# Feed-forward weights kept in DRAM as split pairs: every second tile stored by the first token group, loaded by the second and third

## The chip, the cores and the metric

The kernel runs on one core of one Trainium2 chip. Its time is the device time of an execution in microseconds (us), given as the median of several runs. The core has five engines with a queue each: TensorE (PE, matmuls; the profile keeps its weight loads apart as PEld), VectorE (DVE), ScalarE (ACT), GpSimd (POOL) and SyncE (SP), which issues the transfers (DMAs) between DRAM and the on-chip memory. Each queue runs in order.

## The reference

One layer of a decoder trunk, in float32, over a prompt of 2048 tokens of width 1024 and 8 further samples of one token each. Cut to what matters:

```
h  = rmsnorm(x) * (1 + sc1) + sh1
qkv, z, ..., aq, ak, av, iq, ik, iw = split(h @ w_in)      # 3664 columns
o_gdn = gated delta rule over chunks (from qkv, z, ...)
o_att = attention over the 256 keys per query that an indexer (iq, ik, iw) picks
x  = x + ga1 * (concat(o_gdn, o_att) @ w_out)
h2 = rmsnorm(x) * (1 + sc2) + sh2
gate, up = split(h2 @ w_ffn_in)                            # 1024 x 5632
x  = x + ga2 * ((silu(gate) * up) @ w_ffn_out)             # 2816 x 1024
y  = rmsnorm(x)
```

## The kernel before, in words

**Split products.** The large products keep float32 accuracy by three passes in the faster format float32r: each operand is a pair, the rounded value (hi) and what the rounding lost (lo), and `mm3` (lines 178 to 182) adds hi·hi, hi·lo and lo·hi into one accumulator bank. A weight tile is 128 x 512. `weights` (lines 149 to 169) makes its pair: it loads the raw tile into a buffer `wr` (2 of them, 256 KB), ACT rounds it into the first half of a buffer `wi` (line 163, called the cast here), and DVE subtracts for the second half (line 164); the two together are called a conversion. `wi` has 3 buffers, so the pair for a tile can be made once PE has finished the tile three before it. Each tile gives PE 4 x 3 matmuls of 512 columns. Called with a key, `weights` also stores the finished pair in DRAM, 512 KB, under that key (lines 166 to 168), and on a later call with the same key loads the pair straight into `wi` (lines 153 to 155): no raw tile, no cast, no subtraction. Before the change only the input projection does so: 56 tiles, stored by the first group of tokens and loaded by the other three, 168 loads.

**Groups.** The prompt is cut into 4 groups of 512 tokens. `projects` runs the input projection of the four, with the delta rule beside it; then `ffn` runs once per group. It does the output projection (16 weight tiles, line 1858), the norm, and then for 11 blocks of 256 hidden columns the first feed-forward product (8 tiles each, line 1919, a tile from two raw loads of 128 KB) and, two blocks at a time, the second (44 tiles in all, line 1966): 148 tiles per group. After each run of tiles the four accumulator banks are drained: line 1769 and 1770 for the residual, lines 1934 to 1941 for the gated product. The names there: `d` is a bank, `tm` and `ca` scratch rows, `ah` and `al` the split product, `hh` and `hl` the split hidden rows. The fourth group carries the 8 samples as well (`samp`); its raw tiles are needed by a further matmul (line 1812), and they come from other buffers (`raw`, lines 1798 to 1802).

**What stands beside it.** While the feed-forward groups run, the rest of the attention runs on the same engines: the indexer's scores (line 1626 on PE, 1628 on ACT, 1635 on DVE), the selection (lines 1489 to 1521), softmax and values (lines 1671 to 1724), the loads of their K and V tiles (lines 1667 and 1696), and copies of the paged caches (line 622, on SP).

**What sets the order.** PE's order is written out by a small planner (`weave`, lines 491 to 514): it runs the streams (feed-forward, indexer, attention, samples) step by step, and chooses by an estimate of when DVE and ACT will be done, to which `weights` adds 0.76 and 0.62 for a conversion (line 165). The order of the other queues is made by the scheduler of the build from the resulting program; SP's order is among these.

Of the kernel before, what the change touches and what calls it, by code (L numbers as in the profile page):

```python
# [112 lines left out]
class K:  # L113
# [1637 lines left out]
    def ffn(self, g):  # L1751
# [44 lines left out]
        side, at, ring = deque(), [0, 0], [0]  # L1796
# [6 lines left out]

        def weights(src):
            if not samp:
                return (*self.weights(src), None)
            return self.weights(src, raw=raw)

        def beside(pq, x, wr, start, stop):
# [43 lines left out]
        for hf in range(2):  # L1853
            cs = slice(hf * 512, (hf + 1) * 512)
            pd = D4()
            pq = P("g") if samp else None
            for k in range(KB):
                wh, wl, wr = weights([A["w_out"][0, k * 128:(k + 1) * 128, cs]])
                if samp:
                    beside(pq, sx[:, k, :], wr, k == 0, k == KB - 1)  # L1860
                yield from three(pd, lambda t: oh[:, k, S(t)], lambda t: ol[:, k, S(t)], wh, wl, k, KB - 1)
            for t in range(4):
                gated_add(pd[t], row[:, cs], xt[:, t, cs], hf, t)
                self.squares(ms[:, t, hf:hf + 1], xt[:, t, cs])
            if samp:
                def out(pq=pq, hf=hf, ms=ms):
                    gated_add(pq[:, :128], rws[:, hf], xs[:, hf])
                    self.squares(ms[:, 4, hf:hf + 1], xs[:, hf])
                after(0, 0, out)
# [37 lines left out]
        for p0 in range(0, np_, per):  # L1907
# [5 lines left out]
            for pi, pr in enumerate(prs):  # L1913
# [3 lines left out]
                for k in range(KB):  # L1917
                    kr = slice(k * 128, (k + 1) * 128)
                    wh, wl, wr = weights([A["w_ffn_in"][0, kr, f0:f0 + 256], A["w_ffn_in"][0, kr, FF + f0:FF + f0 + 256]])
                    if samp:  # L1920
                        beside(pq, sx[:, k, :], wr, k == 0, k == KB - 1)
                    for j in range(4):
                        self.mm3(pd[j], wh[:, S(j)], wl[:, S(j)], hh[:, k, :], hl[:, k, :], k == 0, k == KB - 1)
                        yield 3 * MM, 0, bank(j, k, KB - 1, act=0.6)
                    yield from tick()
                    if not pr and k < KB - 2:
                        hidden(k + 2)
                        yield TP, 0, dict(dve=1.5, act=0.6, use="s", need="s" if k < KB - 3 else None)
# [31 lines left out]
            for hf in range(2):  # L1960
                cs = slice(hf * 512, (hf + 1) * 512)
                pd = D4()
                pq = P("g") if samp else None
                for b in range(nf):
                    fr = (p0 * 2 + b) * 128
                    wh, wl, wr = weights([A["w_ffn_out"][0, fr:fr + 128, cs]])
                    if samp:
                        beside(pq, ax[:, b, :], wr, b == 0, b == nf - 1)
                    yield from three(pd, lambda t: ah[b][:, S(t)], lambda t: al[b][:, S(t)], wh, wl, b, nf - 1)
                last = p0 + per >= np_  # L1970
                for t in range(4):
                    gated_add(pd[t], row[:, cs], xt[:, t, cs], last and hf, t)
                    if last:
                        self.squares(ms[:, t, hf:hf + 1], xt[:, t, cs])
                if samp:
                    def out(pq=pq, hf=hf, last=last, ms=ms):
                        gated_add(pq[:, :128], rws[:, hf], xs[:, hf])
                        if last:
                            self.squares(ms[:, 4, hf:hf + 1], xs[:, hf])
                    after(0, 0, out)  # L1980
# [37 lines left out]
```

## Time and profile before

| what | value |
| --- | --- |
| median of 3 runs | 3674.93 us (3673.78 to 3680.48) |
| the profiled execution, its own time | 3680.55 us |
| its span, first to last instruction | 3678.6 us |
| mean granted clock of TensorE | 0.965 |
| PE, DVE, ACT, POOL busy | 3429.4, 2090.6, 1475.8, 599.2 us |
| read from and written to DRAM | 435.49 MB and 124.75 MB |

The page gives busy time by engine and, for each group of like instructions (line, engine, operation, tiles written and read), their count, busy time, mean duration and the idle time of the engine just ahead of them, with what ended it. Further views of the trace list who waited for whom, busy time in chosen stretches of the span, and the instructions in order of time. Times in the timelines are microseconds from the start of the span. In a list of waits a row reads: the waiting engine, tile and line, what it waited for, us in total, times, longest. A rise of PE's busy time is not more work: matmuls overlap, and their durations are longer when the clock is granted at half.

### The profile page before, as it was taken

Reading aid. Unit: us, or ns where it says so; the run is one execution under the profiler, and the core shown is the slowest. Engines: PE = TensorE matmul, PEld = TensorE weight load, DVE = VectorE, ACT = ScalarE, POOL = GpSimd, SP = SyncE. Lnnn points to the kernel's source line nnn. Section 1 sums busy time; section 2 is a strip of 40 time slices with the busy share of each in tenths; the row PEclk is TensorE's granted clock in tenths of the full one; section 3 lists DMA queues with packets and bytes.
Section 4 is the critical chain, followed back from the end, with each engine's and each line's share of the span. In section 5 each row is a group of like instructions: output and inputs, shape, how many; then the busy total and the mean of one; then the engine's idle time right before and its main releaser. Section 6 shows DMA issues by size and latency. Waiting matters only on the chain.

```text
span 3678.6 us, 62998 instructions
## 1 busy us (share of the span) xinstructions
PE 3429.4 (93%) x23441; PEld 2649.0 (72%) x23441; DVE 2090.6 (57%) x4377; ACT 1475.8 (40%) x2868; POOL 599.2 (16%) x548
## 2 busy tenths in 40 slices
PE   7999999999998898999888999999899999899997
PEld 5867778777776776777665677787677777677775
DVE  3656646646644665666667555667666664443434
ACT  3333323323334333344456544564645543322222
POOL 0001000101001023212210122212022112221213
PEclk7999999999999898999998999999999999899998
DMA  6755575575676225455544453335433233432221
GB/s 246 244 204 164 180 243 175 184 241 167 193 262 205 70 94 157 124 167 161 158 153 130 127 174 113 114 98 177 138 91 99 90 103 107 169 107 80 78 82 64
DMA packets 412270, 545.52 MB, mean 148 GB/s; under 512 B 47364, under 2 KB 285225, under 8 KB 411946
## 3 DMA queue, kind: packets, MB, share of 16 engines
q1 hardware_dynamic: 411954, 541.41, 46.2%
q8 instruction: 186, 3.05, 0.3%
q14 instruction: 130, 1.06, 0.1%
HBM read 435.49 MB, written 124.75 MB: 152 GB/s over the span
## 4 chain that ended last, share of the span: by engine, by line
PE 74%; DVE 9%; DMA 7%; ACT 4%; issue 4%; SPq 1%; POOL 0%; DVEq 0%; ACTq 0%; POOLq 0%
PE d L180 18%; PE d L182 16%; PE d L181 16%; PE s L1626 3%; PE g L1688 3%; PE s L1671 2%; DVE wi L164 1%; PE g L1700 1%; DMA wi<-kept 1%; PE g L1812 1%; DMA wr<-in_w_ffn_out_dram 1%; DMA x_d<-xt 1%; PE g L1058 1%; ACT bias L1500 1%; ACT wi L163 1%
## 5 line engine op out<-in xcount | busy, mean ns | idle before, releaser
L180 PE MATMUL d<-hh,wi 128*128 128x512 f32 x1792 | 778.8, 435 | 24.0 <-DVE tm L1769 5.8
L181 PE MATMUL d<-hl,wi 128*128 128x512 f32 x1792 | 710.6, 397 | 7.0 <-DVE hl L415 5.8
L182 PE MATMUL d<-hh,wi 128*128 128x512 f32 x1792 | 710.6, 397 | 0.0
L164 DVE TENSOR_TENSOR wi<-wr,wi 128x512 fp32r<-128x512 f32 x537 | 402.7, 750 | 470.1 <-ACT wi L163 467.4
L163 ACT CAST wi<-wr 128x512 fp32r<-128x512 f32 x537 | 332.3, 619 | 784.5 <-PE d L182 499.2
L180 PEld LDWEIGHTS d<-hh,wi 128*128 128x128 f32 x1792 | 342.0, 191 | 120.9 <-issue 29.4
L182 PEld LDWEIGHTS d<-hh,wi 128*128 128x128 f32 x1792 | 341.6, 191 | 77.8 <-DVE wi L164 0.8
L181 PEld LDWEIGHTS d<-hl,wi 128*128 128x128 f32 x1792 | 343.1, 191 | 75.6 <-DVE hl L415 10.6
L180 PE MATMUL d<-wi,hh 128*128 128x512 f32 x768 | 324.7, 423 | 20.5 <-DMA wi<-kept 13.2
L180 PE MATMUL d<-wi,ah 128*128 128x512 f32 x704 | 301.2, 428 | 8.8 <-ACT ah L1940 5.6
L181 PE MATMUL d<-wi,hh 128*128 128x512 f32 x768 | 302.0, 393 | 1.0 <-DVE wi L164 1.0
L182 PE MATMUL d<-wi,hl 128*128 128x512 f32 x768 | 302.4, 394 | 0.0
L182 PE MATMUL d<-wi,al 128*128 128x512 f32 x704 | 282.2, 401 | 3.2 <-POOL al L1941 2.6
L181 PE MATMUL d<-wi,ah 128*128 128x512 f32 x704 | 282.2, 401 | 0.0
L1941 POOL TENSOR_TENSOR al<-ca,ah 128x512 fp32r<-128x512 f32 x88 | 119.1, 1365 | 844.9 <-ACT ah L1940 608.4
L1635 DVE SCALAR_TENSOR_TENSOR sc<-rl,iw,sc 128x512 f32<-128x512 f32 (+3 forms) x224 | 165.8, 740 | 81.5 <-ACT rl L1628 75.5
L1628 ACT ACTIVATE rl<-s 128x512 f32<-128x512 f32 (+3 forms) x288 | 150.3, 544 | 144.1 <-PE s L1626 136.6
L1770 POOL TENSOR_TENSOR xt<-xt,tm 128x512 f32<-128x512 f32 x96 | 136.5, 1436 | 411.5 <-DVE tm L1769 365.7
L180 PEld LDWEIGHTS d<-wi,hh 128*128 128x128 f32 x768 | 145.2, 189 | 68.7 <-DMA wi<-kept 17.0
L1626 PE MATMUL s<-ik,iqT 128*128 128x512 f32 (+3 forms) x576 | 170.8, 396 | 10.0 <-ACT rl L1628 9.7
L1500 ACT ACTIVATE bias<-sc,sv 128x640 bf16<-128x640 f32 (+11 forms) x120 | 169.7, 1414 | 22.8 <-DVE sv L1502 13.5
L180 PEld LDWEIGHTS d<-wi,ah 128*128 128x128 f32 x704 | 135.2, 192 | 52.6 <-issue 11.0
(532 smaller groups left out, 5587.5 us busy)
## 6 DMA issues: line engine op xcount, KB each, us to landing
wi<-kept SPq DMA_DIRECT2D x168, 512.0 KB, 3.4
wr<-in_w_ffn_in_dram SPq DMA_DIRECT2D x572, 128.0 KB, 2.3
wr<-in_w_ffn_out_dram SPq DMA_DIRECT2D x143, 256.0 KB, 2.6
kept<-wi SPq DMA_DIRECT2D x56, 512.0 KB, 3.4
xt<-in_x_prompt_dram SPq DMA_DIRECT2D x8, 2048.0 KB
row<-in_w_ada_dram SPq DMA_DIRECT2D x32, 512.0 KB, 4.3
wr<-in_w_in_dram SPq DMA_DIRECT2D x56, 256.0 KB, 3.6
kT<-kT_d SPq DMA_DIRECT2D x54, 256.0 KB, 3.0
```

What stands on the lines that cost most here:

```text
L163: nc.scalar.copy(w[:, 0], wr)
L164: nc.vector.tensor_tensor(w[:, 1], wr, w[:, 0].bitcast(F32), op=OP.subtract)
L180: self.o(nc.tensor.matmul(out, wh, xh, start=start, stop=False, **kw))
L181: self.o(nc.tensor.matmul(out, wh, xl, start=False, stop=False, **kw))
L182: self.o(nc.tensor.matmul(out, wl, xh, start=False, stop=stop, **kw))
L1500: nc.scalar.activation(c, s, AF.Sign, bias=t, accum_out=cnt)
L1626: self.o(nc.tensor.matmul(ps[:, :w], iq[:, h, :].bitcast(F32R), B["ikT"][c * 2 + a][:, :w].bitcast(F32R), start=a == 0, stop=a == 1))
L1628: nc.scalar.activation(r[:, :w], ps[:, :w], AF.Relu)
L1635: nc.vector.scalar_tensor_tensor(s, r[:, :w], iw, s, op0=OP.mult, op1=OP.add)
L1688: self.o(nc.tensor.matmul(po[:, :256], V[:, kb % 4, :], PT[:, b * 256:(b + 1) * 256], start=kb == 0, stop=kb == i))
L1770: (nc.vector if soon else nc.gpsimd).tensor_tensor(xt, xt, tm, op=OP.add)
L1941: nc.gpsimd.tensor_tensor(al[b], a, ah[b].bitcast(F32), op=OP.subtract)
```

## The change

The first, second and third feed-forward group count their weight tiles with `ring`. Tiles with an odd number, the first, third and so on, 74 of 148, now get a key that holds the number alone. The number runs anew in each group, and so the first group stores 74 pairs of 512 KB after their conversion, and the second and third load these 74 pairs each (148 loads in place of 148 raw tiles and their conversions). Tiles with an even number and the whole fourth group stay as they are. The loads and stores are issued on SP like the raw ones. Lines behind 1806 move by one.

```
         def weights(src):
             if not samp:
-                return (*self.weights(src), None)
+                ring[0] += 1
+                return (*self.weights(src, ("ffn", ring[0]) if ring[0] % 2 else None), None)
             return self.weights(src, raw=raw)
```

The change moves instructions on every engine, since a tile that is loaded as a pair adds nothing to the planner's estimate for DVE and ACT. On SP, in the third group, where the first feed-forward product has just begun: `wr` are raw tiles, `xt` the residual rows, `kept` a stored pair, the V and oT rows attention's. Before:

```order
L162 DMA wr<-in_w_ffn_in_dram 128x256 x6
L1930 DMA xt<-x_d 128x4x1024
L1696 DMA V<-V_d 128x4x128
L162 DMA wr<-in_w_ffn_in_dram 128x256 x4
L1696 DMA V<-V_d 128x4x128
L1724 DMA oTh_d<-PT 128x2x128
L162 DMA wr<-in_w_ffn_in_dram 128x256 x2
L1724 DMA oTl_d<-oT 128x2x128
L162 DMA wr<-in_w_ffn_in_dram 128x256 x6
L162 DMA wr<-in_w_ffn_out_dram 128x512 x7
```

and after:

```order
L162 DMA wr<-in_w_ffn_in_dram 128x256 x2
L154 DMA wi<-kept 128x1024
L1931 DMA xt<-x_d 128x4x1024
L1696 DMA V<-V_d 128x4x128
L162 DMA wr<-in_w_ffn_in_dram 128x256 x2
L1696 DMA V<-V_d 128x4x128
L154 DMA wi<-kept 128x1024
L1724 DMA oTh_d<-PT 128x2x128
L1724 DMA oTl_d<-oT 128x2x128
L162 DMA wr<-in_w_ffn_in_dram 128x256 x2
L154 DMA wi<-kept 128x1024
L162 DMA wr<-in_w_ffn_out_dram 128x512
```

Every second raw tile has given its place to the load of a pair, and attention's rows stand behind such loads as they stood behind raw ones. The second piece is DVE's queue in the third group, at the sixth of the eleven gated drains (`th` and `ca` two times each; `sc` are steps of the indexer). Before:

```order
L164 TENSOR_TENSOR wi<-wr,wi 128x512
L1935 SCALAR_TENSOR_TENSOR th<-th,d 128x512
L1635 SCALAR_TENSOR_TENSOR sc<-rl,iw,sc 128x512
L1937 SCALAR_TENSOR_TENSOR ca<-th,d 128x512
L1935 SCALAR_TENSOR_TENSOR th<-th,d 128x512
L1635 SCALAR_TENSOR_TENSOR sc<-rl,iw,sc 128x512
L164 TENSOR_TENSOR wi<-wr,wi 128x512
L1937 SCALAR_TENSOR_TENSOR ca<-th,d 128x512
```

and after:

```order
L164 TENSOR_TENSOR wi<-wr,wi 128x512
L1936 SCALAR_TENSOR_TENSOR th<-th,d 128x512
L1635 SCALAR_TENSOR_TENSOR sc<-rl,iw,sc 128x512 x2
L1938 SCALAR_TENSOR_TENSOR ca<-th,d 128x512
L1936 SCALAR_TENSOR_TENSOR th<-th,d 128x512
L1938 SCALAR_TENSOR_TENSOR ca<-th,d 128x512
```

The subtraction between the two products is gone, and both indexer steps stand ahead of the first. The third piece is DVE's queue in the second group, where the second half of the output projection is drained (`tm` and `ca`; `sv` and `sc` belong to a selection, `s` to the samples). Before:

```order
L1769 TENSOR_TENSOR tm<-d,row 128x512
L164 TENSOR_TENSOR wi<-wr,wi 128x512
L1769 TENSOR_TENSOR tm<-d,row 128x512
L1770 TENSOR_TENSOR xt<-xt,tm 128x512
L1769 TENSOR_TENSOR ca<-d,row 128x512 x2
```

and after:

```order
L1769 TENSOR_TENSOR tm<-d,row 128x512
L1633 SCALAR_TENSOR_TENSOR sc,sums<-rl,iw,sc 128x256
L1770 TENSOR_TENSOR xt<-xt,tm 128x512
L1489 TENSOR_REDUCE sv<-sums 128x1
L1492 TENSOR_TENSOR sc<-sc,cf 128x128
L1769 TENSOR_TENSOR tm<-d,row 128x512
L1490 TENSOR_SCALAR sv<-sv 128x1
L1493 MAX sv<-sc 128x8
L1769 TENSOR_TENSOR ca<-d,row 128x512
L1770 TENSOR_TENSOR xt<-xt,tm 128x512
```

The conversion has left this drain, and steps of the indexer and of a selection have come into it.

## Prediction

> **What bounds the kernel now.** First the top of the profile's page: which engine is full.
>
> ```profile
> span 3678.6 us, 62998 instructions
> PE 3429.4 (93%) x23441; PEld 2649.0 (72%) x23441; DVE 2090.6 (57%) x4377; ACT 1475.8 (40%) x2868; POOL 599.2 (16%) x548
> ```
>
> TensorE holds the span. It idles for 3678.6 - 3429.4 = 249 us, and only what shortens or adds such idling can move the end. So I cut the span at the feed-forward groups (the first matmul of each) and read busy time by stretch: the second to fourth projection, then the first, second and third feed-forward group.
>
> ```profile
> 318.00:1161.90 843.90, 787.11 (x8054) 623.39 (x8053) 464.55 (x1206) 284.60 (x695) 65.26 (x70) 0.98 0.62 202
> 1161.90:1873.70 711.80, 638.49 (x4567) 511.67 (x4565) 445.76 (x933) 285.30 (x552) 156.91 (x123) 0.93 0.46 138
> 1873.70:2520.50 646.80, 618.58 (x2889) 469.68 (x2887) 400.01 (x794) 336.57 (x583) 116.18 (x125) 0.98 0.42 129
> 2520.50:3142.90 622.40, 598.85 (x2627) 468.46 (x2625) 382.27 (x701) 307.88 (x504) 118.74 (x87) 0.98 0.37 115
> 1873.70:3142.90 1269.20, 1217.43 (x5513) 938.14 (x5511) 782.29 (x1494) 644.45 (x1087) 234.93 (x212) 0.98 0.39 122
> ```
>
> The columns are length, busy us of PE, PEld, DVE, ACT and POOL, granted clock, DMA share and GB/s. The conversions that the change takes away lie in groups two and three (last row), where PE idles for 1269.2 - 1217.4 = 51.8 us. That is all there is to win from waits. Next, what the conversions cost there, and who waits for them: the groups by line, and then the list of who waited for the subtraction's result.
>
> ```profile
> L164 DVE TENSOR_TENSOR wi<-wr,wi 128x512 fp32r<-128x512 f32 x293 | 226.5, 773 | 218.8 <-ACT wi L163 217.4
> L163 ACT CAST wi<-wr 128x512 fp32r<-128x512 f32 x294 | 181.8, 619 | 356.3 <-PE d L182 305.5 <-DMA wr<-in_w_ffn_in_dram 20.5 <-DMA wr<-in_w_out_dram 15.8
> ```
>
> ```profile
>   PEld d L180: 0.5, 2
>   PEld d L181: 0.5, 2
>   PEld d L182: 0.4, 1
> ```
>
> ACT itself idles 305.5 us ahead of the cast, for a tile that PE has not yet let go: the conversions run ahead of PE, and PE waits directly for them for next to nothing. They matter only as queue neighbours of other work. What PE does wait for in this stretch is the list of waits:
>
> ```profile
> PE g L1700 <- ACT big L1679: 11.1, 4, 5.3
> PE d L180 <- DVE ca L1937: 5.4, 5, 1.9
> PE d L181 <- DVE hl L415: 4.1, 3, 2.8
> PE d L180 <- DVE tm L1769: 4.0, 3, 2.8
> PE s L1671 <- DVE st L1672: 3.7, 4, 1.4
> PE d L182 <- POOL al L1941: 1.9, 2, 0.9
> ```
>
> These are the softmax (big) and, behind it, drains of the accumulator banks (ca, tm) and the hidden rows (hl), all short.
>
> **The change part by part.** *Removed:* 74 of 148 conversions in each of groups two and three, 148 in all: 148 x 0.619 = 92 us of ACT and 148 x 0.773 = 114 us of DVE. Both engines are under 63% busy there (782 and 644 of 1269 us), so of this only what stood ahead of something that PE waited for counts. One such place, from the timelines of POOL, DVE and PE:
>
> ```profile
> 2877.51 1.66 POOL L1941 TENSOR_TENSOR al<-ca,ah 128x512 fp32r<-128x512 f32 x1 [31.87 <-ACT ah L1940]
> 2877.96 1.76 DVE L164 TENSOR_TENSOR wi<-wr,wi 128x512 fp32r<-128x512 f32 x1
> 2879.64 0.67 DVE L1937 SCALAR_TENSOR_TENSOR ca<-th,d 128x512 f32<-128x512 f32 x1
> 2880.37 0.50 PE L180 MATMUL d<-wi,ah 128*128 128x512 f32 x1 [1.87 <-DVE ca L1937]
> ```
>
> A subtraction of 1.76 us stands ahead of the product ca, and PE waits 1.87 us for ca. The order of the changed kernel has no conversion there (the second piece in the section on the change). I went through all waits of PE over 0.3 us in the stretch in this way; there are 36, 48.6 us in all, the first and the last being
>
> ```profile
> 1897.28 0.50 PE L180 MATMUL d<-wi,hh 128*128 128x512 f32 x1 [0.90 <-DVE tm L1769]
> 3129.94 0.79 PE L182 MATMUL d<-wi,al 128*128 128x512 f32 x1 [0.93 <-POOL al L1941]
> ```
>
> and summed the part of each that the removed conversions fill on the engine waited for, during the wait or in the 3 us ahead of it, capped by the wait: 8.4 us. Counting the removed conversions on both engines gives 17.5 us. I take **-8.4**, since each wait names one engine; ends 0 and -17.5. The rest (softmax, selection) has no removed conversion near it.
>
> The subtraction above is over twice as long as its mean, 0.773 us, and overlaps POOL's own subtraction of 1.66 us. The Trainium skill, SBUF — State Buffer, "Who interferes with whom", says that a VectorE instruction with two SBUF inputs contends with a GpSimd instruction that reads SBUF; the row agrees. By that rule the removed subtractions would also free POOL, and PE's waits for al (1.9 us in the list of waits) could go: an estimate of -10.3 for this term in place of -8.4.
>
> *The clock.* A wait is followed by slow matmuls. Behind one of 2.77 us, with the stretch's granted clock below:
>
> ```profile
> 2004.35 0.80 PE L181 MATMUL d<-hl,wi 128*128 128x512 f32 x1 [2.77 <-DVE hl L415]
> 2004.95 0.63 PE L182 MATMUL d<-hh,wi 128*128 128x512 f32 x1
> 2004.00:2009.50 5.50, 5.15 (x12) 4.08 (x13) 5.50 (x16) 0.00 (x0) 0.00 (x0) 0.50 0.90 345
> ```
>
> The mean clock of 0.98 over 1269 us costs about 0.02 x 1269 = 25 us of work. In proportion to the waits (8.4 of 51.8), **-4**; ends 0 and -8.5 (17.5 of 51.8).
>
> *Added in groups two and three:* 148 loads of a 512 KB pair, each in place of a raw load of 256 KB. Issues and landings:
>
> ```profile
> wi<-kept SPq DMA_DIRECT2D x168, 512.0 KB, 3.4
> wr<-in_w_ffn_in_dram SPq DMA_DIRECT2D x572, 128.0 KB, 2.3
> kept<-wi SPq DMA_DIRECT2D x56, 512.0 KB, 3.4
> DMA to landing us min/median/max: 2.9/3.4/7.9
> ```
>
> A raw load waits only for the raw buffer, which the conversion frees early. A kept load goes straight into wi and waits on SP until PE has finished the tile three before. I followed the PE semaphore that each kept load and the rows ahead of it on SP wait for: apart from the very last load, none stands behind a row that waits for a later PE instruction than its own. Behind it on SP stand kT and V loads of attention; SP waits already, mostly for conversions that follow PE:
>
> ```profile
> SPq L162 <- DVE wi L164: 530.1, 220, 7.7
> SPq L1696 <- PE g L1688: 129.5, 36, 14.7
> ```
>
> So the head of the queue changes its reason to wait, not its pace. From the release to its use a kept tile has two tiles of matmuls. Where nothing lies between them, seven tiles take
>
> ```profile
> 3104.97:3124.03 19.06, 19.06 (x86) 15.76 (x84) 7.62 (x10) 4.36 (x7) 4.80 (x4) 1.00 0.34 99
> ```
>
> or 2.72 us each, so the window is at least 5.4 us against a landing of 3.4 us: 2.0 us spare, gone only when a landing is late. The projection is the nearest case: there all tiles of three groups are loaded so, at a DMA share of 0.62, and PE waited
>
> ```profile
> PE d L180 <- DMA wi<-kept: 14.6, 8, 4.0
> ```
>
> 14.6 us for 168 loads; at that rate 148 loads cost 12.9 us. The change adds 148 x 0.26 MB = 38.8 MB to 1269 us, 31 GB/s on 122, so the share stays near 0.5, and every second tile is still raw. I take a third, **+4**; ends 0 and +12.9.
>
> *Added in group one:* 74 stores of 512 KB; no conversion goes away. A store waits for its conversion on DVE, as the raw load two tiles on does already, and it holds the buffer wi until it has landed: 3.4 us against three tiles, 8.2 us. In the projection's first group 56 such stores stood one behind the other, and the tile kept<-wi is named in none of PE's waits. **+1**; ends 0 and +9.9, one more wait for SP's queue like group one's longest, which is
>
> ```profile
> PE g L1239 <- DMA qT<-qT_d: 9.9, 1, 9.9
> ```
>
> *Moved:* a loaded tile books no time on DVE and ACT with the planner (line 165 is not reached), so index and selection steps come somewhat earlier in groups two and three. In the third piece of the section on the change steps of the indexer and of a selection stand inside a drain where one conversion stood; its maximum takes 1.5 us, against 0.77 for a conversion:
>
> ```profile
> L1493 DVE MAX8 sv<-sc x12: 829/1546/2295, 1449.3 to 2915.9; 128x8 f32<-128x640 f32 x1, 128x8 f32<-128x768 f32 x1, 128x8 f32<-128x896 f32 x1, 128x8 f32<-128x1024 f32 x1
> ```
>
> Elsewhere it takes work out of drains. **+2**; ends -4 and +6, four such drains at 1.5 us, with the gain for the side on which steps leave a drain bounded by the 4.0 us of waits for tm.
>
> Sum: -8.4 - 4 + 4 + 1 + 2 = -5.4 us, so **-5**. The profiled execution took 3680.55 us (span 3678.6 and 1.95 around it), 5.6 above the median of the runs; the difference goes onto the median: 3674.93 - 5 = **3670**. About 0.2%, 7.3 us, is what a measurement of this kernel can tell from no change.
>
> **The rivals.** *The engines' queues count more than I allow (faster).* Half the conversions gone shorten each drain on both engines: -17.5, the clock's -8.5, then +4 and +1: -21, or **3654**. For it speaks that no conversion is left between the products of the second piece; against it, that most of the 48.6 us are softmax and selection with no conversion near. The Trainium skill, TensorE: Matmul & The Clock Gate, "Part 1: The HAM clock gate (the "warmup" mystery)", says the array's default is the half clock, and a busy window of about 3.4 us releases it; the slow rows behind the wait agree, and by it short waits that vanish would give back more than their own length. Chance 0.34.
>
> *Kept loads come late (slower).* Place: tiles loaded in groups two and three where matmuls run back to back. The price is the projection's rate, 12.9 us, in 8 x 148/168 = 7 waits; each puts PE at half clock for some 3.4 to 5.5 us (the row at 2004 shows 5.5), losing 1.7 us or more: 12 us. With the moved steps at +6, the stores at +1 and the gain of 8.4 without its clock: 12.9 + 12 + 6 + 1 - 8.4 = +23; with the moved steps at nothing +17, and I take that: **3692**. It decides once waits for wi<-kept, clock included, pass 8.4 + 4 + 7 = 19 us. For it speaks the maximum landing of 7.9 us against a window of 5.4; against it the lower DMA share. Chance 0.25.
>
> **How the numbers follow.** My forecast, within 7.3 us of no change, has 0.41, the faster rival 0.34, the slower one 0.25; so faster 0.34, same 0.41, slower 0.25. The likeliest case alone reaches from 3668 to 3682. The range goes on to both rivals, a little beyond the faster one and short of the slower one's full price: 3650 to 3690.
>
> **What would show it.** Right: waits for wi<-kept in groups two and three under 8 us; L164 down by 148 (537 to 389 on wr); PE's waits for ca, tm, hl and th lower by some 8 us; group one's length within 5 us of 711.8; the fourth group unchanged. Wrong: over 15 us of waits for wi<-kept, or PE waiting in group one for a conversion held up by a store; or, on the other side, idle time in groups two and three falling from 52 to under 30 us.

## The result, and the profile after

| | before | after |
| --- | --- | --- |
| median of 4 runs each | 3674.36 us (3669.31 to 3680.48) | 3703.93 us (3699.57 to 3706.17) |
| ratio after to before | | 1.0078, 95% interval 1.0062 to 1.0093 |
| span of the profiled execution | 3678.6 us | 3704.4 us |

The change makes the kernel slower by some 29 us, 0.8%. The forecast was -5, and the measured median lies above its range. The top of the page of after:

```profile
span 3704.4 us, 62595 instructions
PE 3427.9 (93%) x23441; PEld 2650.1 (72%) x23441; DVE 1980.8 (53%) x4229; ACT 1393.3 (38%) x2720; POOL 585.9 (16%) x548
```

DVE lost 110 us of work and ACT 82 (the prediction counted 114 and 92), and PE's busy time is the same within 2 us. So the 25.8 us between the two spans are idle time of PE. The same three feed-forward groups as in the prediction, by stretch (length, busy time of PE, PEld, DVE, ACT and POOL, granted clock, DMA share, GB/s):

```profile
1161.60:1894.69 733.09, 638.41 (x4566) 509.40 (x4565) 443.56 (x931) 283.90 (x550) 155.83 (x123) 0.93 0.58 186
1894.69:2548.40 653.71, 625.36 (x2933) 472.38 (x2932) 362.56 (x758) 306.72 (x532) 116.40 (x126) 0.99 0.50 160
2548.40:3168.63 620.23, 587.67 (x2584) 465.16 (x2582) 311.84 (x592) 256.50 (x412) 106.99 (x86) 0.97 0.44 143
```

Group one, which gained the stores and lost nothing, went from 711.8 to 733.1 us: +21.3, with PE busy for the same 638.4. Group two went from 646.8 to 653.7 and group three from 622.4 to 620.2, together +4.7. These two are best read together: some 44 matmuls have moved from group three into group two (2889 became 2933 there, and 2627 became 2584), and PE's busy time with them. Most of the loss is in group one. Its DMA share rose from 0.46 to 0.58. The groups of the conversion in the page of after:

```profile
L164 DVE TENSOR_TENSOR wi<-wr,wi 128x512 fp32r<-128x512 f32 x389 | 282.6, 727 | 505.2 <-ACT wi L163 479.4
L163 ACT CAST wi<-wr 128x512 fp32r<-128x512 f32 x389 | 240.9, 619 | 711.3 <-PE d L182 425.2
```

The count is the 389 that was foretold, and ACT still idles for PE (425.2 us): the conversions stayed ahead of it. What PE waited for in groups two and three of after (us in total, times, longest):

```profile
PE d L180 <- DMA wi<-kept: 9.8, 3, 7.3
...
PE d L181 <- DVE hl L415: 6.8, 4, 2.0
...
PE d L180 <- DVE ca L1938: 3.9, 3, 1.7
...
PE d L180 <- DVE th L1936: 2.8, 2, 1.5
...
PE d L180 <- DVE ca L1769: 1.9, 2, 1.4
...
PE d L180 <- DVE tm L1769: 1.0, 1, 1.0
```

The stored pairs came late 3 times. The wait for ca at the gated drains fell from 5.4 to 3.9 and that for tm from 4.0 to 1.0, but that for hl rose from 4.1 to 6.8. For group one, the longest entries of PE's waits in the second part of the group, 1395 to 1880, first in before:

```profile
PE g L1688 <- ACT PT L1703: 13.9, 4, 4.7
PE g L1239 <- DMA qT<-qT_d: 9.9, 1, 9.9
...
PE g L1294 <- DVE s L1289: 4.2, 2, 3.3
...
PE d L180 <- DVE tm L1769: 2.7, 4, 1.3
```

and in after:

```profile
PE g L1688 <- ACT PT L1703: 16.8, 3, 8.9
PE g L1239 <- DMA iqT<-iqT_d: 12.8, 1, 12.8
...
PE g L1294 <- DVE s L1289: 7.3, 4, 3.8
PE d L180 <- DVE tm L1769: 4.9, 5, 1.7
...
PE d L180 <- DVE st L1678: 3.7, 1, 3.7
```

One short wait is new, the last row (3.7 us, for a step of the softmax); the other rows are each some 2 to 3 us longer. No wait of PE in this window names a conversion or a stored pair. That picture fits many causes, so the runs below take them apart.

### The profile page after: what moved, and what is told of

It is laid out like the page before. It is cut to its first block, busy times and chain, and to the rows that moved or that the text cites. A ratio compares the mean times of both kernels' runs of the same rounds, so it can differ in the third digit from the quotient of the medians.

```text
span 3704.4 us, 62595 instructions
## 1 busy us (share of the span) xinstructions
PE 3427.9 (93%) x23441; PEld 2650.1 (72%) x23441; DVE 1980.8 (53%) x4229; ACT 1393.3 (38%) x2720; POOL 585.9 (16%) x548
## 3 DMA queue, kind: packets, MB, share of 16 engines
q1 hardware_dynamic: 409938, 619.00, 51.1%
## 4 chain that ended last, share of the span: by engine, by line
PE 74%; DMA 9%; DVE 8%; issue 3%; ACT 3%; SPq 2%; POOL 0%; DVEq 0%; ACTq 0%; POOLq 0%
PE d L180 18%; PE d L182 16%; PE d L181 16%; PE s L1626 3%; PE g L1688 3%; PE s L1671 3%; DMA wi<-kept 2%; DMA wr<-in_w_ffn_in_dram 2%; PE g L1700 1%; PE g L1813 1%; DVE wi L164 1%; PE g L1058 1%; DMA x_d<-xt 1%; ACT wi L163 1%; DMA wr<-in_w_ffn_out_dram 1%
## 5 line engine op out<-in xcount | busy, mean ns | idle before, releaser
L164 DVE TENSOR_TENSOR wi<-wr,wi 128x512 fp32r<-128x512 f32 x389 | 282.6, 727 | 505.2 <-ACT wi L163 479.4
L163 ACT CAST wi<-wr 128x512 fp32r<-128x512 f32 x389 | 240.9, 619 | 711.3 <-PE d L182 425.2
L1942 POOL TENSOR_TENSOR al<-ca,ah 128x512 fp32r<-128x512 f32 x88 | 118.4, 1356 | 912.4 <-ACT ah L1941 672.5
L1500 ACT ACTIVATE bias<-sc,sv 128x640 bf16<-128x640 f32 (+11 forms) x120 | 169.7, 1414 | 38.8 <-DVE sv L1502 19.0
```

Of the source, the lines that this page charges most:

```text
L163: nc.scalar.copy(w[:, 0], wr)
L164: nc.vector.tensor_tensor(w[:, 1], wr, w[:, 0].bitcast(F32), op=OP.subtract)
L1500: nc.scalar.activation(c, s, AF.Sign, bias=t, accum_out=cnt)
L1942: nc.gpsimd.tensor_tensor(al[b], a, ah[b].bitcast(F32), op=OP.subtract)
```

## The experiments

The theories, by the letters that the expectations use. **A**: the issues of the 74 stores crowd SP's queue. **B**: the bytes of the stores crowd the transfers. **C**: a store holds its buffer `wi` too long. **D**: the order of the instructions, which the change moved, is worse. All times are medians; "before" is run beside each kernel on the same chip. Group lengths are of the profiled executions.

**The stores alone, and the loads alone.** The stores of group one without any loads:

```
- ("ffn", ring[0]) if ring[0] % 2 else None
+ ("ffn", ring[0]) if ring[0] % 2 and not g else None
```

> The first group stores its 74 pairs, and nobody loads them: groups two and three convert all tiles as before. Theory A (SP's queue is full in the first feed-forward group, between about 1395 and 1840 us, because the page copies run there; each store issued on it puts back every load behind it): the first group is longer by some 20 us, as in the changed kernel, groups two and three are as before, total +18 to +25 us over before. Theory B (bytes: the stores' traffic makes the loads of the first group land later) and theory C (a store holds its buffer wi until it has landed, so the next conversions are late): the same +20. Theory D (the loss comes from the new order of index and selection steps that the planner makes once loaded tiles book no time): under +5 us, since here every tile books its time.

3699.07 us against 3669.4, ratio 1.0085 (1.0068 to 1.0102). The whole loss is here, and every tile is booked with the planner as before, so D is not needed for it. Its first two groups, by stretch:

```profile
1155.78:1889.28 733.50, 642.27 (x4566) 511.23 (x4565) 445.41 (x933) 284.68 (x552) 155.56 (x123) 0.93 0.58 186
...
1889.28:2532.47 643.19, 616.58 (x2890) 468.26 (x2888) 400.14 (x794) 335.61 (x581) 115.84 (x125) 0.99 0.41 129
```

Group one is as long as in after, and group two is as before. The other half, no stores, the loads from pairs that the projection has stored:

```
- ("ffn", ring[0]) if ring[0] % 2 else None
+ list(self.kept)[ring[0] // 2 % 56] if ring[0] % 2 and g else None
```

> No store in the feed-forward groups: groups two and three load, for every second tile, one of the 56 pairs that the projection has stored (another matrix's values, the same transfer), so that the feed-forward result is another one. Theories A, B, C: the first group is as before (712 us), and groups two and three together are within 8 us of before, total within 10 us of before. Theory D: most of the loss stays, total +15 to +25 us, with groups two and three longer.

3676.89 against 3669.4, ratio 1.0016 (1.0006 to 1.0027): the 148 loads, with the conversions that they spare, cost a little and gain nothing.

**Issues or bytes.** Each store as two halves, in the whole change (twice the issues, the same bytes):

```
+ for a in range(2):
+     nc.sync.dma_start(self.kept[key][:, a], w[:, a].bitcast(F32))
```

> The changed kernel with each of the 74 stores of the first group issued as two halves of 256 KB: the same bytes, twice the issues. Theory A: the first group grows by about as much again as the change made it grow, 20 us, since SP has to issue 74 more; total about +45 to +50 us over before. Theories B and C: the bytes and the landings are the same, so the total stays at the changed kernel's +29, within 6 us.

3703.37 against 3669.4, ratio 1.0098 (1.0081 to 1.0115), a loss of 34 us where the change itself loses 29. Twice the issues hardly cost more in all. By stretch the loss lies elsewhere, though: group one took 722.4 us here and group two 662.4, where after has 733.1 and 653.7. The stores issued from ACT's queue, with the whole change:

```
- nc.sync.dma_start(self.kept[key], w.bitcast(F32))
+ (nc.scalar if key[0] == "ffn" else nc.sync).dma_start(self.kept[key], w.bitcast(F32))
```

> The changed kernel with the 74 stores issued from ACT's queue in place of SP's: the same bytes and the same buffers held. Theory A: the first group falls back to within 6 us of before's 712 us, and the total is 18 to 25 us under the changed kernel, within 10 us of before. Theories B and C: the first group stays near 733 us and the total near the changed kernel's. Against A also speaks a price on ACT: 74 issues there, each some half us, with a wait for the subtraction in ACT's queue.

3693.68 against 3669.4, ratio 1.0064 (1.0047 to 1.0081). Some 24 us of loss stay with no store on SP's queue, some 7 of them by the loads, as loads_only has it. But group one took 721.1 us, 9.3 more than before in place of 21.3. That is neither what A expected (within 6 us of 712) nor what B and C did (near 733), so this run alone does not clear SP's queue. Then the stores cut to 16 and to 64 of the 128 partitions, without loads (an eighth and a half of the bytes, the same issues):

```
+ nc.sync.dma_start(self.kept[key][0:16], w[0:16].bitcast(F32))
```

> As stores_only (74 stores in the first feed-forward group, no loads), but each store writes 16 of the 128 partitions: the same number of issues and waits on SP, an eighth of the bytes. Stores_only cost +29.7 us. Theory A (SP's time per issue and its waits, among the page copies): still +20 to +30. Theory B (the bytes: all loads of the stretch land later beside 38.8 MB of stores): +0 to +8, an eighth of 29.7 being 3.7. If both hold, the value between tells the shares.

> As stores_only, each store writing 64 of the 128 partitions: the same issues, half the bytes. Theory A: still +25 to +30. Theory B: about half, +15. Between the two lies a sum of both.

An eighth: 3676.29 against 3677.61, ratio 1.0000 (0.9988 to 1.0013). Half: 3689.72, ratio 1.0042 (1.0023 to 1.0061). Group one by stretch, with an eighth of the bytes:

```profile
1159.97:1874.71 714.74, 636.71 (x4567) 509.68 (x4565) 446.53 (x933) 285.26 (x552) 157.62 (x123) 0.93 0.49 144
```

and with half of them:

```profile
1153.63:1883.31 729.68, 639.06 (x4566) 510.01 (x4565) 449.10 (x933) 284.82 (x552) 157.44 (x123) 0.93 0.55 161
```

+3, +18 and, with all bytes, +22 us of group one. 74 issues on SP by themselves cost nothing, so A alone does not explain the loss: the bytes of the stores are needed for it.

**Another group.** The second group stores, the third loads:

```
- ("ffn", ring[0]) if ring[0] % 2 else None
+ ("ffn", ring[0]) if ring[0] % 2 and g else None
```

> The change put off by one group: the second feed-forward group stores its 74 pairs, where no page copies run, and only the third loads them. Theories A and B, both of which lay the loss to the first group's full SP queue and DMA engines: the first group is as before; the 74 stores in the second group cost little, under +8; the third group's 74 loads cost half of what loads_only showed (+7.5), so about +4: total +2 to +12. If stores cost the same wherever they stand: +30 or more.

3679.43 against 3677.61, ratio 1.0012 (1.0001 to 1.0022), with the 74 loads of group three in it. The same 38.8 MB cost next to nothing in group two, which took 646.5 us against 646.8: group one has something that makes it vulnerable. Among what stands there and nowhere else are the 192 page copies of line 622 (they start from 1416.9 to 1804.4). In `stores_only` the part of group one ahead of them took 269.3 us, against 268.1 before, with 25 of the 74 stores in it; the two parts behind it are 12.8 and 7.7 us longer. C is out as well, since buffers and conversions are the same in both groups.

**The page copies on another queue.** The kernel before, with the page copies issued from POOL:

```
- pg = nc.sync.value_load(pt_i[0:1, i:i + 1], min_val=0, max_val=n_phys - 1)
+ pg = nc.gpsimd.value_load(pt_i[0:1, i:i + 1], min_val=0, max_val=n_phys - 1)
...
- nc.sync.dma_start(to, src[ds(pg, 1)].rearrange("a t c -> (a t) c"))
+ nc.gpsimd.dma_start(to, src[ds(pg, 1)].rearrange("a t c -> (a t) c"))
```

> The kernel before, with the 192 page copies (line 622) issued from POOL's queue in place of SP's; nothing is stored or loaded as a pair. If SP is the queue that holds the first feed-forward group up (theory A), the group (712 us before) gets shorter by 5 to 20 us even without the change, and SP is idle for a good part of 1395 to 1840 us. If the bytes do (theory B), it stays within 5 us.

3765.25 against 3677.61, ratio 1.0241 (1.0218 to 1.0264). Group one grew to 800.1 us, where A expected it 5 to 20 us shorter. The copies stand among POOL's own steps, and PE's largest wait is for a step of DVE (59.7 us in 7 waits for `s`, line 1296) that itself waits 41.1 us for POOL. So this says nothing on the stores.

**With and without page copies.** Now the questions are: **E**, the copies' bytes meet the stores' bytes; **F**, the copies keep SP's queue full, so that loads go out without a lead and any delay of a transfer reaches PE; **G**, the page copies have no part in it. Two bases, and on top of each the stores as in `stores_only`. In `pages_none` 24 plain copies take the place of the 192 (the scheduler put them at 36 to 92 us, ahead of most of the projection, where they lengthen the first projection group by some 40 us; that is outside the stretch in question and in both kernels of the pair). In `pages_tiny` the 192 copies by the table are back in group one with an eighth of their bytes. The plain copies of both, and the small ones of `pages_tiny`:

```
+ to = dst[s // 2, :, :, s % 2, :] if dst is self.ikp_d else dst[s]
+ self.nc.sync.dma_start(to, src[s * NPAGE:s * NPAGE + NPAGE].rearrange("g t c -> t g c"))
...
- nc.sync.dma_start(to, src[ds(pg, 1)].rearrange("a t c -> (a t) c"))
+ nc.sync.dma_start(to[0:16], src[ds(pg, 1), 0:16].rearrange("a t c -> (a t) c"))
```

> The kernel before without the 192 page copies in group one: the caches are copied in the second projection group by 24 plain copies, pages in order rather than by the table, so the samples' attention works on other pages. It is the base of the next kernel. All theories: the stretch of the page copies has SP free and a lower DMA share; the time moves by up to 20 us either way, since some 38 MB of traffic move into the projection.

> pages_none with the 74 stores of group one and no loads. Theory E (the stores' bytes cost because the page copies' bytes are on the transfer engines beside them): the difference to pages_none is under 8 us. Theory F (they cost because the page copies keep SP's queue full, so that loads go out without a lead and any longer landing hits PE): under 8 us as well. Theory G (the stores cost by themselves, with group one's own loads): 25 to 35 us, as with the page copies.

> pages_none with the 192 page copies by the table back in group one, each of 16 of the 128 rows, an eighth of the bytes: SP's queue is as full as before, the transfer engines are not. It is the base of the next kernel. Theory F: group one takes as long as before. Theory E: group one is shorter, like in pages_none.

> pages_tiny with the 74 stores of group one and no loads. Difference to pages_tiny: theory E under 8 us, theory F 15 us or more, theory G 25 to 35 us.

Without the copies the stores cost nothing: 3691.28 against 3692.25 (1.0048, 1.0031 to 1.0066, against 1.0047, 1.0028 to 1.0066, both to before). With an eighth of the copies' bytes they cost all: 3744.42 against 3715.64 (1.0187, 1.0163 to 1.0211, against 1.0112, 1.0094 to 1.0130), 29 us. In these four kernels the samples' attention works on other pages of the caches than the table names. Group one by stretch in pages_none:

```profile
1202.72:1887.15 684.43, 627.81 (x4566) 505.10 (x4564) 446.93 (x933) 285.11 (x552) 158.78 (x123) 0.94 0.37 116
```

in pages_none_stores:

```profile
1201.56:1886.79 685.23, 625.65 (x4567) 503.22 (x4565) 447.86 (x933) 284.78 (x552) 158.48 (x123) 0.95 0.52 171
```

in pages_tiny:

```profile
1207.96:1914.74 706.78, 634.81 (x4566) 509.01 (x4565) 447.31 (x933) 285.27 (x552) 157.46 (x123) 0.94 0.37 116
```

and in pages_tiny_stores:

```profile
1208.35:1940.40 732.05, 640.73 (x4567) 512.11 (x4564) 444.19 (x933) 284.84 (x552) 157.18 (x123) 0.93 0.50 163
```

The first and third have the same DMA share, 0.37, and so have, nearly, the second and fourth, 0.52 and 0.50. Yet the stores add 0.8 us to the one and 25.3 to the other. Page bytes and the share of the transfer engines don't decide; E and G fall. What differs, beside the 192 small transfers themselves, is SP. Its waits for the conversion from 1450 to 1800 in pages_none:

```profile
SPq L162 <- DVE wi L164: 130.0, 60, 4.6
```

in pages_none_stores, where line 168 is the store:

```profile
SPq L168 <- DVE wi L164: 76.8, 32, 4.4
SPq L162 <- DVE wi L164: 48.3, 29, 4.2
```

in before:

```profile
SPq L162 <- DVE wi L164: 5.3, 11, 1.1
```

and in pages_tiny_stores:

```profile
SPq L168 <- DVE wi L164: 4.2, 4, 2.4
...
SPq L162 <- DVE wi L164: 0.3, 1, 0.3
```

In pages_tiny itself the two are 3.2 us. Where SP waits some 125 to 130 us of 350 for conversions, it has reached its loads before they may go out. Where it waits for 5 or less, loads go out only when their turn comes, and a delay is not made up; this last is an argument, and no row shows it. ACT's idle time ahead of the cast, for raw tiles that had not landed, from 1395 to 1880, bears on it. First pages_none and pages_none_stores:

```profile
ACT wi L163 <- DMA wr<-in_w_ffn_in_dram: 20.7, 8, 4.1
...
ACT wi L163 <- DMA wr<-in_w_ffn_in_dram: 49.6, 18, 4.8
```

then pages_tiny and pages_tiny_stores:

```profile
ACT wi L163 <- DMA wr<-in_w_ffn_in_dram: 59.5, 24, 4.3
...
ACT wi L163 <- DMA wr<-in_w_ffn_in_dram: 83.1, 31, 5.1
```

In both pairs ACT waits longer for raw tiles with the stores, by 29 and 24 us in this row, but only in the second does PE lose time. The same row differs by 18 us between before (79.8) and loads_only (61.7), where group one is the same, so this is a hint and not more. SP's reads of the page numbers in before, with the first and last start:

```profile
L620 SPq TENSOR_LOAD <-pt_i x192: 262/270/742, 1415.9 to 1803.7; - x192
```

and in stores_only:

```profile
L620 SPq TENSOR_LOAD <-pt_i x192: 262/273/1187, 1412.8 to 1855.3; - x192
```

The stretch in which SP has no pause grows from 388 to 443 us. That growth is no measure of the loss, though. With an eighth of the stores' bytes, in stores_tiny, the row is

```profile
L623 SPq TENSOR_LOAD <-pt_i x192: 262/272/714, 1415.1 to 1838.0; - x192
```

or 423 us, and group one is only 3 us longer. In stores_act, with no store on SP, it is 422 us.

**Relief for SP, with all bytes.** The K and V copies of a page from one read of its number (64 reads fewer), alone and with the change on top:

```
+ for both in ((ik,), (k, v)):
...
      pg = nc.sync.value_load(pt_i[0:1, i:i + 1], min_val=0, max_val=n_phys - 1)
+     for dst, src in both:
...
          nc.sync.dma_start(to, src[ds(pg, 1)].rearrange("a t c -> (a t) c"))
```

> The kernel before, with the K and V page copies of one page issued one behind the other from one read of the page's number: 64 of the 192 reads on SP with their register work are gone, all copies and their bytes stay. Theory F (in group one SP's queue is the bound of the loads, since the page copies fill it): SP has 64 x 0.75 = 48 us less to do in its stretch without a pause, and group one, 711.8 us before, gets 5 to 15 us shorter. Theory E (the bytes count): no change.

> The whole change with the page copies of pair. Theory F: SP gets back 48 us of the some 55 that the stores add to its stretch, so that the difference to pair is 10 to 20 us, and to the kernel before 0 to 15, in place of 29. Theory E: 29 us above pair.

3672.32 against 3674.09, ratio 0.9988 (0.9978 to 0.9999), and 3697.45, ratio 1.0057 (1.0042 to 1.0072): 25 us between them. SP waits 31.1 us for conversions in pair and 3.0 in pair_after, so the change took the room again. But both of F's expectations failed: group one of pair, 712.3 us, is no shorter than before, and 25 us is more than the 10 to 20 foretold, nearer to E's 29. A room of 31 us did not shield PE from the stores. One number read for eight copies (168 reads fewer; the samples then work on other pages), and the stores on top:

```
+ if not g:
      pg = nc.sync.value_load(pt_i[0:1, i:i + 1], min_val=0, max_val=n_phys - 1)
```

> The kernel before, where the page's number is read once for eight copies: the 192 page copies keep their bytes and their issues in group one, 168 of 192 reads with their register work are gone (each copy of a set of eight takes the same page, so the samples' attention works on other pages). It is the base of the next kernel. Theory F: SP gets 168 x 0.75 = 126 us of room and waits for conversions again by over 60 us from 1450 to 1800; group one 5 to 25 us under 711.8, unless the copies, now closer together, hold the loads back all the same. Theory E: no change.

> eight with the 74 stores of group one and no loads. Difference to eight: theory F under 10 us, since SP has room again, with the bytes of copies and stores all there; theory E (bytes on the transfer engines) 25 us or more.

3661.16 against 3673.93, ratio 0.9966 (0.9955 to 0.9977), and 3678.56, ratio 1.0013 (1.0000 to 1.0026): 17 us between them, between the two expectations. The two later parts of group one tell more. In eight:

```profile
1423.75:1694.11 270.36, 248.74 (x1149) 200.80 (x1148) 174.61 (x409) 111.78 (x222) 77.45 (x51) 0.96 0.59 172
1694.11:1859.30 165.19, 148.59 (x634) 114.40 (x632) 112.11 (x230) 89.10 (x171) 31.84 (x26) 0.94 0.41 136
```

and in eight_stores:

```profile
1430.81:1712.70 281.89, 250.22 (x1150) 200.96 (x1148) 173.34 (x409) 111.70 (x222) 76.02 (x51) 0.95 0.72 227
1712.70:1877.93 165.23, 149.60 (x634) 115.12 (x632) 112.52 (x230) 89.18 (x171) 31.73 (x26) 0.94 0.55 183
```

The scheduler packed the shorter copies closer, so that the last one started at 1644.6 in eight and at 1684.3 in eight_stores, ahead of the second row. In the first row, with the copies, the stores cost 11.5 us; in the second, without them, 0.04 us at a DMA share of 0.55. While the copies run in eight, from 1417 to 1646, SP waits 2.5 us for conversions; in its second row it waits 69.4. One pair of kernels shows both cases.

**The whole change with the copies elsewhere.** The 192 copies by the table issued in the projection (they fell between 42 and 450 us):

```
+ if g == 1:
+     with self.tc.high_priority(offset=-LATE):
+         self.copy_pages()
  run = self.project(g, rows)
```

> The kernel before with all 192 page copies by the table issued in the projection's first two groups, where SP waits for conversions, and none in group one. Theory F: group one as in pages_none, some 685 us in place of 711.8; what the projection loses by it is open, 0 to 30 us.

> The whole change with the page copies of early. Theory F: the stores cost under 5 us, so that the difference to early is that of the loads alone, 3 to 12 us, in place of 29. Theory E says the same here, since the bytes are gone from group one as well; against theory G, by which the stores cost 25 us or more anyway.

3717.26 (ratio 1.0120, 1.0103 to 1.0138) and 3719.03 (1.0118, 1.0101 to 1.0134): the projection loses more than group one wins (62 us, where 0 to 30 were expected, against 27), but the whole change on top costs 2 us, in place of 29. Group one is 685.0 us in early, and in early_after

```profile
1226.44:1914.59 688.15, 626.00 (x4567) 504.07 (x4564) 446.93 (x931) 283.58 (x550) 158.56 (x123) 0.95 0.52 171
```

**What follows.** The 38.8 MB of stores cost PE's time only beside the 192 page copies on SP, whatever the bytes of the copies; there their cost grows with their own bytes, and the issues alone add nothing. Both conditions are shown. That it is SP's lack of a pause which makes the copies count, and not the small transfers themselves, is argued from SP's waits: in every run here the two come together, except in pair, where SP had 31 us of waits for conversions and the change still cost 25 us. How the bytes then act is argued as well: loads without a lead land later beside more traffic, and PE's waits grow by 2 to 3 us each. The traces with the stores hold no landing times of these loads, so this step stays open. A kernel that fills SP's queue without any transfer, with and without the stores, would tell the two apart; none was run. None of the kernels with the whole change is faster than before. pair, the page copies alone made cheaper, is not slower.

## Why the prediction was wrong, point by point

**The step that failed** is "Added in group one: 74 stores of 512 KB", put at +1 with ends 0 and +9.9. It measured +21.3 in group one's length, and in the medians stores_only loses 29.7 us, as much as the whole change. The terms for groups two and three, -6.4 together, came to +4.7. The step asked whether the store holds the buffer `wi` too long; it does not, as the prediction said, and PE waited for no conversion because of a store. It did not ask what the stores' bytes do to the other loads of group one, and whether these had a lead. Its comparison was the projection's first group, where 56 such stores stood and none of PE's waits names them. SP's list of waits there, in before:

```profile
SPq L168 <- DVE wi L164: 115.5, 40, 9.4
```

SP waited 115.5 of 318 us for conversions, against 5.3 of 350 in the second part of group one. The projection was a case with room and without page copies, and the prediction took it for a like one. That row, beside the 5.3, was to be had from the trace of before. The upper end, "one more wait for SP's queue like group one's longest", named the right queue, but counted one wait where several grew.

**The gain in groups two and three** (-8.4, and -4 of clock) did not come. PE's idle time there was 51.8 us before; in after it is 653.71 - 625.36 + 620.23 - 587.67 = 60.9, and 51.1 without the waits for stored pairs. The waits for ca, tm, th and hl were to fall by 8; they went from 5.4 + 4.0 + 3.0 + 4.1 = 16.5 in the same rows to 3.9 + 1.0 + 2.8 + 6.8 = 14.5. A conversion that stood ahead of a step in the queue was mostly not what that step was late for. The waits for al, which could go by the rule of the Trainium skill (SBUF — State Buffer, "Who interferes with whom") once fewer subtractions run beside POOL, are at 1.3 us, from 1.9; POOL's subtractions for al take 1356 ns in the mean of the whole kernel, from 1365, so the rule shows little here.

**The kept loads** (+4, ends 0 and +12.9) cost 9.8 us of waits, inside the ends and above the 8 us that were to show the step right. The rate of the projection was the better estimate. **The moved steps** (+2) can't be told from nothing: groups two and three together are within 1 us in early and early_after (1270.1 and 1270.6), though work did move from the third to the second.

**The rivals.** The faster one fell with the gain. The slower one had the right sign by another cause: it wanted 19 us from waits for `wi<-kept`, which gave half of that. The foretold sign of error, "PE waiting in group one for a conversion held up by a store", named the right group with the wrong mechanism; "group one's length within 5 us of 711.8" did its work, since the 733.1 showed at once where to look.

## What to carry to other kernels

Before a transfer is called hidden, look at what its issuing queue waits for in that very stretch. In this kernel a queue with 130 us of waits for its consumers took 74 stores of 512 KB for 1 us, and with next to none the same stores cost 25 us; 31 us of such waits, in pair, were not enough. A DMA share of 0.5 says neither. And a stretch that serves as a comparison must agree with the one in question in what its queues wait for, not in the number of transfers alone.

## What the runs showed of the hardware

At a DMA share of 0.52 over 685 us, PE lost nothing to 38.8 MB of added stores. The bytes of the page copies cost little beside the copies themselves: group one took 706.8 us with an eighth of the bytes, 711.8 with all and 684.4 without the copies. Issued from POOL in place of SP, the 192 copies made the kernel 2.4% slower.
